# RWKV's low-rank products in fp32r on 128 stacked rows, and part of the down weights' sums made in the score stage of a hybrid GDN/RWKV-7 block

## The chip, the cores and the metric

One core of one Trainium2 chip (trn2). The metric is device time in microseconds of one launch; lower is better. The profile comes from one execution of its own, read by the hardware profiler; the times come from other runs without it.

## The reference, cut to what matters

One layer of an encoder on 512 tokens of width 2048, all in fp32. A norm and one input projection feed two groups of mixers, gated DeltaNet (8 heads of 128) and RWKV-7 (16 heads of 64); then an output projection, cross attention to 256 memory tokens, and an MLP of width 8192 with squared ReLU.

```python
xn = rmsnorm(h); y = xn @ w_in
mixed = concat(gdn_group(y[..., :GDN_COLS]), rwkv_group(y[..., GDN_COLS:]))
h = h + mixed @ w_out
h = h + cross_attention(rmsnorm(h), rmsnorm(mem))
h = h + square(relu(rmsnorm(h) @ mlp_w_up)) @ mlp_w_down
out = rmsnorm(h)
# in rwkv_group: y is mixed with its shifted self, then
w_log = -softplus(-(w0 + tanh(w_lo) @ w2)) - 0.5     # w_lo: 64 columns of y, w2: 64 x 1024
a = sigmoid(a0 + a_lo @ a2)                          # a_lo: 64 columns of y, a2: 64 x 1024
g = sigmoid(g_lo) @ g2
```

## The kernel before, in words

Nearly all large products are made in fp32r, a form of fp32 with fewer bits that TensorE takes at a higher rate. An operand is split into a high part (a cast on ACT) and a low part (a subtraction on DVE), and three products (high by high, high by low, low by high) are added up in PSUM. Small products of the mixers stay in fp32.

The stages follow each other on PE: input projection in 59 blocks of 128 columns (tiles `py`), with the mixers' small products between; key products `kp` and `kq`; value products `vp`, `vo`; output projection `op` (a Strassen form with 7 products); scores `sc`; attention `at`; up (tiles with u at the end) and down (with d at the end), both in the seven-product form too.

In the mixers, and again in up and down, the order of all instructions is written out by hand: chains of work (generators) yield operations, and a planner issues the one that its costs and due times put first (`cost`, `start`, `issue`, `run`). In between (output projection, scores, attention) the program is written straight and the framework's scheduler orders each engine's queue.

RWKV works in 8 head pairs, `rwkv(j)`. Its front end makes two products of 64 rows, `pW` (w2's columns of the pair by tanh(w_lo)) and `pA` (a2's by a_lo): `lw` holds w2 on rows 0 to 63 and a2 on rows 64 to 127, and `wa` the two activations likewise. `rows()` makes `wa` once, from block 0 of the projection. Tiles of one tag share buffers: `sr` has two, `E1`, `tA` and the others one. `rs` are the small products of the recurrence along the eight chunks of 64 tokens.

The seven-product form of down needs four sums of weight blocks (s1 to s4) in 13 groups of 2048 columns; the sums of three more groups are made in place by `insitu`, and `splits` cuts them. `presum` fetches the four blocks A11, A21, A22, A12 of a piece, makes the sums on DVE and stores them to HBM (`Sd`); `todo` and `upto` hold what is left. Most groups are made beside the mixers in pieces of 410 columns (tiles `ds`); `remaining` makes the rest beside up and down in buffers that stand free there (`ab`, `h`, `sl`, `acc`). Down's loads fetch the sums from HBM.

The score stage has two halves g of eight steps n2. A step loads 1024 columns (`kqr`, two DMAs of 256 KB), splits them into `kqh` and `kql` (three buffers each of load and split), and makes 24 products. In the first half each of six steps also splits two blocks of the normed input (`second`); in the second half the first half's softmax and its transposes lie between. Attention's first two loads (`VOd`) follow.

Of the kernel before, what the change touches and what calls it, by code (L numbers as in the profile page):

```python
# [9 lines left out]
F32 = mybir.dt.float32  # L10
F32R = mybir.dt.float32r
# [6 lines left out]
P = 128  # L18
# [6 lines left out]

CST = {}
_off = 0
for _n, _w in (("ident", 128), ("ones", 128), ("mA", 128),
               ("lv64", 2 * 64), ("cen", 64), ("sneg", 128), ("mbias", 128),
               ("rst64", 512)):  # L30
    CST[_n] = (_off, _w)
    _off += _w
# [13 lines left out]
def constants():  # L46
    c = np.zeros((P, NCST), np.float32)

    def put(name, a):
        o, w = CST[name]  # L50
        c[:, o:o + w] = a

    i = np.arange(P)
    put("ident", np.eye(P))
    put("ones", 1.0)
    j = np.arange(64)
    st = (j[:, None] < j[None, :]).astype(np.float32)
    inc = (j[:, None] <= j[None, :]).astype(np.float32)
    put("mA", np.tile(np.concatenate([st, inc], 1), (2, 1)))

    def level(n, s):
        a = np.arange(n)
        blk = a[:, None] // (2 * s) == a[None, :] // (2 * s)
        return (blk & (a[:, None] % (2 * s) >= s) & (a[None, :] % (2 * s) < s)).astype(np.float32)

    put("lv64", np.concatenate([np.tile(level(64, 16 << l), (2, 1)) for l in range(2)], 1))
    put("cen", np.tile(np.eye(64) - 1.0 / 64, (2, 1)))
    put("sneg", -(i[:, None] < i[None, :]).astype(np.float32))
    put("mbias", np.where(i[:, None] <= i[None, :], 1e30, -1e30))
    put("rst64", np.tile((np.arange(512) % 64 != 0).astype(np.float32), (P, 1)))  # L70
    return c


def build(tc, I, out):
# [12 lines left out]

    prm = pc.tile([P, NPRM], F32, name="prm")
    nc.sync.dma_start(prm, I["prm"])
    NC0 = 256  # L90
    cst0 = pc.tile([P, NC0], F32, name="cst0")
    cst = pq.tile([P, NCST - NC0], F32, name="cst")

    def K(name):
        o, w = CST[name]
        return cst0[:, o:o + w] if o < NC0 else cst[:, o - NC0:o - NC0 + w]

# [5 lines left out]
        o, w = PRM[name]  # L103
        return prm[:, o:o + w]

    ident, ones = K("ident"), K("ones")

    def cbias(v, nm):
        t = pc.tile([P, 1], F32, name=f"cb_{nm}")
# [172 lines left out]
    def after(*ev):  # L282
        return lambda: ev in events
# [236 lines left out]
    dp = pq.tile([P, 28], F32, name="dp")  # L520
    omu, nA = dp[:, 0:27], dp[:, 27:28]
    hw0, ha0, hka, hgnw, hconv = (cols(n) for n in ("w0", "a0", "ka", "gnw", "conv"))
    onesr = pq.tile([P, P], F32R, name="onesr")
    bonesr = pq.tile([P, P], F32R, name="bonesr")

    def derived():
        yield DV.tensor_scalar(out=omu, in0=cols("mu"), scalar1=-1.0, scalar2=1.0, op0=ALU.mult, op1=ALU.add)
        for t in (hw0, ha0, hka, hgnw, hconv):
            yield DV.tensor_scalar(out=t, in0=t, scalar1=0.5, scalar2=None, op0=ALU.mult)
        yield after("consts")  # L530
        yield DV.tensor_copy(onesr, ones)
        yield DV.memset(bonesr.bitcast(F32), 0.0)
        for h in (slice(0, 64), slice(64, 128)):
            yield DV.tensor_copy(bonesr[h, h], ones[h, h])
# [126 lines left out]
        yfree.append(ys.pop(n))  # L661


    wa = pq.tile([P, T], F32, name="wa")
    sgh, sgl, sst = (pq.tile([P, T], F32R, name=n) for n in ("sgh", "sgl", "sst"))
    RT = pq.tile([P, 4, 3, 8], F32, name="RT")
    Rd = pd.tile([64, T], F32, name="Rd", tag="Rd")
# [1 line left out]
    def rows():  # L669
        R = tl("gE")  # L670
        yield DV.memset(R, 0.0)
        rs128 = tl("bon")
        g8 = slice(32, 40)
        b8 = slice(64, 72)
        yield after("rstd")
        yield AC.activation(nA, col("alog"), AF.Exp)
        yield DV.tensor_scalar(out=nA, in0=nA, scalar1=-1.0, scalar2=None, op0=ALU.mult)
        yield DV.memset(rs128[g8, :], 1.0)
        for c in range(4):
            yield DV.memset(rs128[g8, c * P:c * P + 1], 0.0)  # L680
        yield after("derived")
        yield from shiftmix(0, 0, wa)
        yield AC.activation(wa[0:64, :], wa[0:64, :], AF.Tanh)
        sg1, y2 = tl("gAq"), tl("gkt")
        yield from shiftmix(1, 1, sg1)
        yield AC.activation(sg1, sg1, AF.Tanh, scale=0.5)
        yield DV.tensor_scalar(out=sg1, in0=sg1, scalar1=0.5, scalar2=0.5, op0=ALU.mult, op1=ALU.add)
        yield from split_(sg1, sgh, sgl)
        events.add(("lowrank",))
        yield from shiftmix(2, 2, y2)  # L690
        yield AC.activation(y2[0:32, :], y2[0:32, :], AF.Tanh, scale=0.5)
        yield AC.activation(R[b8, :], y2[b8, :], AF.Tanh, scale=0.5)
        yield DV.tensor_scalar(out=y2[0:32, :], in0=y2[0:32, :], scalar1=0.5, scalar2=0.5,
                               op0=ALU.mult, op1=ALU.add)

        yield AC.copy(sst[0:32, :], y2[0:32, :])
        yield AC.copy(sst[64:96, :], y2[0:32, :])
        yield DV.tensor_tensor(out=y2[0:32, :], in0=y2[0:32, :], in1=sst[0:32, :].bitcast(F32), op=ALU.subtract)
        yield AC.copy(sst[32:64, :], y2[0:32, :])
        x_, e_ = short(t="st"), tl("gkn")  # L700
        yield DV.tensor_scalar(out=x_[g8, :], in0=y2[g8, :], scalar1=col("dtb")[g8, :], scalar2=None, op0=ALU.add)
        yield DV.scalar_tensor_tensor(out=e_[g8, :], in0=x_[g8, :], scalar=-1.0, in1=x_[g8, :],
                                      op0=ALU.mult, op1=ALU.min)
        yield AC.activation(e_[g8, :], e_[g8, :], AF.Exp)
        yield AC.activation(e_[g8, :], e_[g8, :], AF.Ln, bias=b_one[g8, :])
        yield DV.scalar_tensor_tensor(out=x_[g8, :], in0=x_[g8, :], scalar=0.0, in1=e_[g8, :],
                                      op0=ALU.max, op1=ALU.add)
        yield DV.tensor_scalar(out=x_[g8, :], in0=x_[g8, :], scalar1=nA[g8, :], scalar2=None, op0=ALU.mult)
        yield DV.tensor_tensor_scan(out=R[g8, :], data0=rs128[g8, :], data1=x_[g8, :], initial=0.0,
                                    op0=ALU.mult, op1=ALU.add)  # L710
        R3 = R.rearrange("p (c t) -> p c t", t=P)
        tail = tl("gqn")
        t3 = tail.rearrange("p (c t) -> p c t", t=P)
        yield DV.tensor_tensor(out=t3[g8], in0=R3[g8, :, P - 1:P].broadcast_to([8, 4, P]),
                               in1=R3[g8], op=ALU.subtract)
        yield AC.activation(R[96:104, :], tail[g8, :], AF.Exp)
        yield DV.tensor_scalar(out=R[b8, :], in0=R[b8, :], scalar1=0.5, scalar2=0.5, op0=ALU.mult, op1=ALU.add)
        pt = psb("prt", "scg", 1)
        for c in range(4):
            yield TE.transpose(pt[:, c * P:(c + 1) * P], R[:, c * P:(c + 1) * P], ident)  # L720
        yield SY.dma_start(Rd, R[32:96, :])
        yield DV.tensor_copy(RT, pt.rearrange("p (c a b) -> p c a b", a=4, b=32)[:, :, 1:4, 0:8])
# [135 lines left out]
    def rwkv(j):  # L858
        base = 3 + 7 * j
        js = slice(j * P, (j + 1) * P)  # L860
        lw = tl("lw", P)
        yield SM.dma_start(lw, I["w2a2"][:, js])
        c3 = lambda a: a.rearrange("p (c t) -> p c t", t=64)
        yield after("lowrank")
        yield after("zeros")
        pW, pA = psb(f"pW{j}"), psb(f"pA{j}")
        yield [TE.matmul(pW, lw[0:64, :], wa[0:64, :], start=True, stop=True),
               TE.matmul(pA, lw[64:128, :], wa[64:128, :], start=True, stop=True)]
        tw = short()
        yield AC.activation(tw, pW, AF.Tanh, scale=0.5, bias=hw0[:, j:j + 1])  # L870
        tA = tl("tA")
# [811 lines left out]
    def turned():  # L1683
        g, _, probs = turn.pop(0)
        for e in range(2):
            for mt in range(2):
# [4 lines left out]
                S.copy(phi[kk], pt)  # L1691
                V.tensor_tensor(out=plo[kk], in0=pt, in1=phi[kk].bitcast(F32), op=ALU.subtract)

    for g in range(2):
        banks = (("mm", 2), ("mg", 2), ("mg", 2), ("mm", 2)), (("scr", 1), ("scg", 1), ("mx", 2), ("mx", 2))
        pts = [psb(f"sc{g}_{t}", *banks[g][t]) for t in range(4)]
        for n2 in range(8):
# [3 lines left out]
                nc.sync.dma_start(raw[:, i * 512:(i + 1) * 512], KQd[2 * n2 + i][:, g * 512:(g + 1) * 512])  # L1701
            wh = pw.tile([P, 1024], F32R, tag="whi", name=f"kqh{cnt[0]}", bufs=NWS)
            wl = pw.tile([P, 1024], F32R, tag="wlo", name=f"kql{cnt[0]}", bufs=NWS)
            split(raw, wh, wl)
            if g == 0 and n2 < 6:
                second(2 * n2 + 4)
                second(2 * n2 + 5)
# [15 lines left out]
        if g == 1:  # L1723
            for n in range(2):
                begun.append((psb(f"at{n}", "mg"), *wload(VOd[0][:, :, n * P:(n + 1) * P])))
                attend(*begun[n], 0)
        turn.append((g, pts, []))
        if g == 1:
            for t in range(4):
# [203 lines left out]
    def splits():  # L1933
        for u in units:
            if u[0] == "d" and u[1:3] in INSITU and u[1:] not in PRE:
                for i, w in order_of(u):
                    for x in xs(u):
# [2 lines left out]
                        halves[u, i, x] = hl = yield from take(hfree)  # L1940
                        yield from cut(r, *hl)
                        events.add(("half", u, i, x))
                        if w not in (A11, "s2") and (w != A12 or u == units[-1]):
                            wfree.append(r)
                continue
# [422 lines left out]
def layout(inputs):  # L2368
# [53 lines left out]
    put("alog", a["gdn_A_log"][0].reshape(8, 1), slice(32, 40))  # L2422
    d["prm"] = prm
    d["cst"] = constants()
    d["w2a2"] = np.concatenate([a["rwkv_w2"][0], a["rwkv_a2"][0]], 0)
    g2 = a["rwkv_g2"][0]
    d["g2a"] = np.ascontiguousarray(g2[:128])
    d["g2b"] = np.ascontiguousarray(g2[128:])
# [37 lines left out]
```

## Time and profile before

| | |
|---|---|
| runs | 2888.92, 2887.84, 2888.71 us; median 2888.71 |
| profiled execution | span 2890.0 us from the first to the last instruction; this is the time of it that is on hand, 1.3 above the median of the runs |
| busy | PE 2862.2, PEld 2419.1, DVE 2333.9, ACT 1571.7, POOL 214.7 us |
| DMA | 553.01 MB, mean 191 GB/s |
| granted TensorE clock | 0.999 |
| first and last start on PE | py 6.8 to 907.0; sc 1455.3 to 1544.9; at 1545.2 to 1634.5; first up product 1634.8 |

PE makes the products and PEld loads their weights beside it. A row of a group has the line, engine, operation, tiles as out<-in, shapes and count, then busy time and mean length in ns, then the engine's idle time ahead of it and who ended that. L257 is the planner's helper that records every operation, L122 the helper for products outside it; so rows are told apart by tiles. Rows in order of time have the start, the length, the engine and the operation; SPq is the queue of DMA issues. A row of waits has who waited for whom, the total in us, the count and the longest.

### The profile page before, as it was taken

To read this page: it belongs to the slowest core of one execution; us is meant where nothing else is said; L and a number is where in the kernel's file an instruction comes from. 1 tells how busy PE (TensorE), PEld (TensorE's weight loads), DVE (VectorE), ACT (ScalarE), POOL (GpSimd) and SP (SyncE) were. 2 spreads that over 40 slices of the span, in tenths; PEclk is the share of its full clock that TensorE was granted. 3 is DMA by queue.
4 is the path that set the end of the run, shared out by engine and by line. 5 is a ranking of instruction groups with operands and counts; after the bars stand their busy time and mean duration, and the time that the engine had idled before them with its cause. 6 is when DMAs were issued, how large, how long until landed. Compare 5 with 4: busy or idle time off the path is not lost.

```text
span 2890.0 us, 49168 instructions
## 1 busy us (share of the span) xinstructions
PE 2862.2 (99%) x18794; PEld 2419.1 (84%) x18794; DVE 2333.9 (81%) x3559; ACT 1571.7 (54%) x2233; POOL 214.7 (7%) x539
## 2 busy tenths in 40 slices
PE   9999999999999999999999999999999999999998
PEld 7877887877877888889988888888888888888887
DVE  7787787787877877769956898899998878786888
ACT  6555555645656655664445556555555644454544
POOL 0213213213212100000000000000000000000000
PEclk9999999999999999999999999999999999999999
DMA  5656656657656788784422354666565878887733
GB/s 191 166 147 176 176 149 187 165 154 189 180 161 200 214 257 274 232 292 151 124 95 88 110 164 153 199 195 207 189 200 178 292 249 277 295 257 247 265 101 110
DMA packets 321212, 553.01 MB, mean 191 GB/s; under 512 B 101128, under 2 KB 188428, under 8 KB 320976
## 3 DMA queue, kind: packets, MB, share of 16 engines
q1 hardware_dynamic: 293584, 518.41, 58.7%
q10 hardware_dynamic: 27392, 31.46, 3.1%
q8 instruction: 147, 2.41, 0.3%
q14 instruction: 89, 0.73, 0.1%
HBM read 443.45 MB, written 106.31 MB: 190 GB/s over the span
## 4 chain that ended last, share of the span: by engine, by line
PE 94%; DMA 3%; DVE 1%; ACT 1%; issue 1%; ACTq 0%; SPq 0%; DVEq 0%
PE py L257 22%; PE mxu L257 12%; PE mgd L257 6%; PE mgu L257 6%; PE mxd L257 6%; PE op L122 6%; PE vp L122 3%; PE mmu L257 3%; PE sc L122 3%; PE at L122 3%; PE scrd L257 3%; PE scgd L257 3%; PE mmd L257 3%; PE kq L257 3%; PE kp L257 2%; DMA wraw<-in_wo 1%
## 5 line engine op out<-in xcount | busy, mean ns | idle before, releaser
L257 ACT CAST whi<-wraw 128x1024 fp32r<-128x1024 f32 (+1 forms) x365 | 382.8, 1049 | 370.1 <-PE py L257 138.7
L257 DVE TENSOR_TENSOR wlo<-wraw,whi 128x1024 fp32r<-128x1024 f32 (+1 forms) x365 | 446.8, 1224 | 90.0 <-ACT whi L257 82.5
L257 PE MATMUL py<-xhi,whi 128*128 128x512 f32 x928 | 373.9, 403 | 6.8 <-ACT xhi L257 6.8
L257 PE MATMUL py<-xhi,wlo 128*128 128x512 f32 x928 | 373.1, 402 | 0.0
L257 PE MATMUL py<-xlo,whi 128*128 128x512 f32 x928 | 372.4, 401 | 0.0
L257 ACT CAST whi<-w 128x1024 fp32r<-128x1024 f32 x178 | 187.6, 1054 | 174.0 <-PE scgd L257 42.3
L257 DVE TENSOR_TENSOR wlo<-w,whi 128x1024 fp32r<-128x1024 f32 x178 | 217.3, 1221 | 43.4 <-ACT whi L257 40.9
L257 PE MATMUL mxu<-cb,whi 128*128 128x512 f32 x1016 | 249.3, 392 | 0.0
L257 PEld LDWEIGHTS mxu<-cb,whi 128*128 128x128 f32 x1016 | 184.7, 189 | 34.3
L257 PEld LDWEIGHTS py<-xhi,whi 128*128 128x128 f32 x928 | 175.3, 189 | 42.0 <-ACT xhi L257 6.8
L257 PEld LDWEIGHTS py<-xhi,wlo 128*128 128x128 f32 x928 | 175.3, 189 | 34.7 <-issue 1.0
L257 PEld LDWEIGHTS py<-xlo,whi 128*128 128x128 f32 x928 | 175.3, 189 | 33.8 <-DVE xlo L257 0.5
L131 DVE TENSOR_TENSOR wlo<-wraw,whi 128x1024 fp32r<-128x1024 f32 x112 | 136.7, 1222 | 44.8 <-ACT whi L130 44.3
L130 ACT CAST whi<-wraw 128x1024 fp32r<-128x1024 f32 x112 | 117.6, 1051 | 86.8 <-PE op L122 26.2
L257 PE MATMUL mxu<-cb,wlo 128*128 128x256 f32 x1016 | 142.7, 283 | 0.7 <-DVE wlo L257 0.7
L257 PEld LDWEIGHTS mxu<-cb,wlo 128*128 128x128 f32 x1016 | 135.1, 191 | 6.0 <-DVE wlo L257 0.9
L257 PE MATMUL mgu<-cb,whi 128*128 128x512 f32 x512 | 129.3, 394 | 0.1
L257 PE MATMUL mxd<-whi,cb 128*128 128x512 f32 x512 | 126.8, 389 | 0.0
L257 PE MATMUL mgd<-whi,cb 128*128 128x512 f32 x512 | 126.4, 389 | 0.0
L257 ACT ACT_TABLE_LOAD x87 | 111.6, 1283 | 16.5 <-DVE suml_gon L257 8.6
L122 PE MATMUL op<-ob,whi 128*128 128x256 f32 (+1 forms) x752 | 115.2, 304 | 0.0
L257 ACT CAST whi<-ws 128x1024 fp32r<-128x1024 f32 x75 | 79.0, 1053 | 64.0 <-PE mgu L257 48.1
(943 smaller groups left out, 6429.3 us busy)
## 6 DMA issues: line engine op xcount, KB each, us to landing
wraw<-in_w_in SPq DMA_DIRECT2D x116, 512.0 KB, 4.7
wraw<-in_w_up SPq DMA_DIRECT2D x65, 512.0 KB, 3.6
w<-in_w_up SPq DMA_DIRECT2D x63, 512.0 KB, 4.2
ds<-in_w_dm SPq DMA_DIRECT2D x128, 205.0 KB, 4.4
sd_s<-ds SPq DMA_DIRECT2D x128, 205.0 KB, 4.9
wraw<-sd_s SPq DMA_DIRECT2D x51, 512.0 KB, 4.9
w<-sd_s SPq DMA_DIRECT2D x50, 512.0 KB, 5.5
w<-in_w_dm SPq DMA_DIRECT2D x48, 512.0 KB, 4.9
```

What stands on the lines that cost most here:

```text
L122: PE.matmul(o, l, r, start=start, stop=stop, skip_group_check=again)
L130: S.copy(hi, src)
L131: V.tensor_tensor(out=lo, in0=src, in1=hi.bitcast(F32), op=ALU.subtract)
L257: f(*a, **k)
```

## The change

Three things change. The low-rank operands are split: `xw2` holds the high part of tanh(w_lo) on rows 0 to 63 and its low part on rows 64 to 127, `xa2` the same for a_lo with the halves swapped. The weights are sent twice on the rows (`w2a2` now 128 x 2 x 1024 with w2 and a2 beside each other), and each pair splits its 256 columns into `lhl`. For pW and for pA two fp32r products of 128 rows are added up: low weights, then high weights. `lw` moves into E1's buffer, `wa` into tA's, `lhl` into one of sr's.

Second, the score stage makes up to fifteen pieces of 256 columns of the sums that are left: `fetched` loads, `summed` adds one step later, `stored` writes them in the step after. `remaining` finds fewer left.

Third, smaller edits: the constant of ones is written by a memset into the fp32r tile `onesr` and no longer loaded, and in the in-situ units the buffer of s1 is given back only after s2 is made.

```diff
@@ constants @@
-for _n, _w in (("ident", 128), ("ones", 128), ("mA", 128),
+for _n, _w in (("ident", 128), ("mA", 128),
...
-    NC0 = 256
+    NC0 = 128
...
-    ident, ones = K("ident"), K("ones")
+    ident = K("ident")
+    onesr = pc.tile([P, P], F32R, name="onesr")
+    ones = onesr.bitcast(F32)
+    V.memset(ones, 1.0)
...
-        yield DV.tensor_copy(onesr, ones)
@@ rows @@
-    wa = pq.tile([P, T], F32, name="wa")
+    xw2, xa2 = (pq.tile([P, T], F32R, name=n) for n in ("xw2", "xa2"))
...
+        wa = tl("tA")
+        lo64, up64 = slice(0, 64), slice(64, 128)
         yield from shiftmix(0, 0, wa)
-        yield AC.activation(wa[0:64, :], wa[0:64, :], AF.Tanh)
+        yield AC.activation(wa[lo64, :], wa[lo64, :], AF.Tanh)
+        for X, p, q in ((xw2, lo64, up64), (xa2, up64, lo64)):
+            yield AC.copy(X[p, :], wa[p, :])
+            yield DV.tensor_tensor(out=X[q, :], in0=wa[p, :], in1=X[p, :].bitcast(F32), op=ALU.subtract)
@@ rwkv @@
-        lw = tl("lw", P)
-        yield SM.dma_start(lw, I["w2a2"][:, js])
+        lw = tl("E1", shape=[P, 8, 65]).rearrange("p a b -> p (a b)")[:, 0:2 * P]
+        yield SM.dma_start(lw.rearrange("p (a b) -> p a b", b=P), I["w2a2"][:, :, js])
...
-        yield [TE.matmul(pW, lw[0:64, :], wa[0:64, :], start=True, stop=True),
-               TE.matmul(pA, lw[64:128, :], wa[64:128, :], start=True, stop=True)]
+        lhl = tile_of(pm, [P, 512], F32R, "sr", f"lhl_{cnt[0]}", NSH["sr"])
+        yield from split_(lw, lhl[:, 0:2 * P], lhl[:, 2 * P:4 * P])
+        for i, (pt, X) in enumerate(((pW, xw2), (pA, xa2))):
+            for s in (1, 0):
+                yield TE.matmul(pt, lhl[:, (2 * s + i) * P:(2 * s + i + 1) * P], X, start=s == 1, stop=s == 0)
@@ scores @@
+    spans = [(e, m, c, min(c + M, 2048)) for e, m in todo for c in range(upto.get((e, m, "s4"), 0), 2048, M)]
+    held, made_ = [], []
+    def fetched(s):
+        e, m, c, n = spans.pop(0)
+        b = [pl.tile([P, M], F32, tag=f"ds{i}", name=f"ds{s}_{i}", bufs=2)[:, 0:n - c] for i in range(4)]
+        for i in (A21, A22, A11, A12):
+            nc.sync.dma_start(b[i], I["w_dm"][e, m][i][:, c:n])
+        held.append((e, m, c, n, b))
+    def summed():
+        e, m, c, n, (a11, a21, a22, a12) = held.pop(0)
+        for j, o, x, y, op in (("s1", a22, a21, a22, ALU.add), ("s3", a21, a11, a21, ALU.subtract),
+                               ("s2", a11, a22, a11, ALU.subtract), ("s4", a12, a12, a11, ALU.subtract)):
+            V.tensor_tensor(out=o, in0=x, in1=y, op=op)
+            made_.append((Sd[e, m, j][:, c:n], o))
+            upto[e, m, j] = n
+        if n == 2048:
+            todo.remove((e, m))
+    def stored():
+        while made_:
+            nc.sync.dma_start(*made_.pop(0))
...
+            stored()
+            if g * 8 + n2 < 15:
+                fetched(g * 8 + n2)
             split(raw, wh, wl)
+            if g * 8 + n2:
+                summed()
...
                 attend(*begun[n], 0)
+            stored()
@@ splits, in-situ units @@
+                        if w == "s1":
+                            yield after("sum", u, "s2", x)
@@ layout @@
-    d["w2a2"] = np.concatenate([a["rwkv_w2"][0], a["rwkv_a2"][0]], 0)
+    w2a2 = np.stack([a["rwkv_w2"][0], a["rwkv_a2"][0]], 1)
+    d["w2a2"] = np.concatenate([w2a2, w2a2], 0)
```

More of the change, by code (lines that the diff above doesn't have):

```diff
@@ L54, in constants @@
     put("ident", np.eye(P))
-    put("ones", 1.0)
     j = np.arange(64)
@@ L522, in build @@
     hw0, ha0, hka, hgnw, hconv = (cols(n) for n in ("w0", "a0", "ka", "gnw", "conv"))
-    onesr = pq.tile([P, P], F32R, name="onesr")
     bonesr = pq.tile([P, P], F32R, name="bonesr")
@@ L866, in rwkv @@
         pW, pA = psb(f"pW{j}"), psb(f"pA{j}")
-        yield [TE.matmul(pW, lw[0:64, :], wa[0:64, :], start=True, stop=True),
-               TE.matmul(pA, lw[64:128, :], wa[64:128, :], start=True, stop=True)]
+        cnt[0] += 1
+        lhl = tile_of(pm, [P, 512], F32R, "sr", f"lhl_{cnt[0]}", NSH["sr"])
[3 more added lines that the diff above has]
+                yield TE.matmul(pt, lhl[:, (2 * s + i) * P:(2 * s + i + 1) * P], X, start=s == 1, stop=s == 0)
         tw = short()
```

## The prediction

> **What bounds the kernel now.** I read the table of busy time by stage first, then the waits of PE, then the order of time around the products that change, then DVE and SP in the score stage.
>
> The table's columns are stretch, length, then busy time and instructions of PE, PEld, DVE, ACT and POOL, the granted clock, the DMA share and GB/s. The eight stretches are mixers with input projection, key products, value products, output projection, scores, attention, up, down.
>
> ```profile
> 0.00:907.00 907.00, 897.84 (x7882) 719.72 (x7883) 706.48 (x1305) 502.67 (x708) 199.33 (x508) 1.00 0.62 172
> ...
> 1118.00:1295.50 177.50, 176.55 (x896) 150.73 (x897) 123.27 (x199) 109.27 (x181) 0.00 (x0) 1.00 0.80 261
> ...
> 1455.20:1545.10 89.90, 89.90 (x410) 74.63 (x410) 37.86 (x61) 32.75 (x54) 0.00 (x0) 1.00 0.31 98
> ...
> 1634.60:2271.00 636.40, 635.61 (x3789) 566.10 (x3788) 572.64 (x761) 361.98 (x507) 0.00 (x0) 1.00 0.59 185
> 2271.00:2890.00 619.00, 608.83 (x2687) 503.79 (x2685) 504.49 (x607) 310.11 (x379) 0.00 (x0) 0.99 0.71 234
> ```
>
> PE is busy to within 1 us in every stretch but the first and the last (start and tail of the kernel), at clock 1.00. DVE is 90% busy in the up stage and 42% in the score stage. A busy PE can still hide waits, so the waits of PE come next, first to 1120 us, then from there to the end:
>
> ```profile
> PE py L257 <- ACT xhi L257: 6.8, 1, 6.8
> PE kp L257 <- DVE wlo L257: 2.7, 1, 2.7
> PE rs L257 <- DVE Qs L257: 2.2, 2, 1.2
> PE gs L257 <- DVE TtG L257: 1.2, 1, 1.2
> PE kq L257 <- DVE y L257: 1.1, 1, 1.1
> ...
> PE mxu L257 <- DVE wlo L257: 0.7, 1, 0.7
> PE vo L122 <- DVE wlo L131: 0.7, 1, 0.7
> PE at L122 <- ACT phi L1691: 0.2, 1, 0.2
> ```
>
> The last three are all there is after 1120 us: 1.6 us, of which 0.7 in up, none in down, none in the score stage. So PE's own instructions set the end. Work taken from DVE or from the DMA queues gains at most these few us; work given to them costs nothing until PE waits.
>
> **The low-rank products.** PE in order of time (start, length) at the first head pair and at the third:
>
> ```profile
> 58.37 0.39 PE L257 MATMUL py<-xlo,whi 128*128 128x512 f32 x1
> 58.69 0.69 PE L257 MATMUL pW<-wa,lw 64*128 64x512 f32 x1
> 58.70 0.69 PE L257 MATMUL pA<-wa,lw 64*128 64x512 f32 x1
> 59.22 0.59 PE L257 MATMUL pW<-wa,lw 64*128 64x512 f32 x1
> 59.23 0.59 PE L257 MATMUL pA<-wa,lw 64*128 64x512 f32 x1
> 59.75 0.50 PE L257 MATMUL py<-xhi,wlo 128*128 128x512 f32 x1
> 60.08 0.39 PE L257 MATMUL py<-xhi,whi 128*128 128x512 f32 x1
> 60.31 0.40 PE L257 MATMUL py<-xlo,whi 128*128 128x512 f32 x1
> ...
> 266.84 0.69 PE L257 MATMUL pW<-wa,lw 64*128 64x512 f32 x1
> ...
> 267.90 0.43 PE L257 MATMUL rs<-BK,BTz 128*128 128x64 f32 x2
> 268.15 0.48 PE L257 MATMUL py<-xhi,whi 128*128 128x512 f32 x1
> 268.46 0.39 PE L257 MATMUL py<-xlo,whi 128*128 128x512 f32 x1
> ```
>
> An fp32 product stands as two records. pW and pA start 10 ns apart, so they run together on the two halves of the rows. Neighbouring py start 0.23 us apart (60.08 to 60.31) though each record lasts 0.39: a full fp32r product of 512 columns costs 0.23 of PE's time, its length overlaps. From 58.37 to 60.08 there would be two such intervals without the visit, 0.46; it took 1.71, so the visit costs 1.25. The third visit, between small fp32 products, costs at least the 1.06 from 266.84 to 267.90.
>
> New: four fp32r products of 128 rows and 512 columns, 4 x 0.23 = 0.92. Beside small fp32 products the first one pays what py pays at 268.15, 0.31 instead of 0.23, so 1.00. The saving is 0.06 at worst (1.06 - 1.00) and 0.33 at best (1.25 - 0.92); over 8 head pairs 0.5 to 2.6 us. I take 0.3 per visit, 2.4 us: nearest the first visit, since the fp32r quartet fits between py without a switch on either side.
>
> The Trainium skill, "TensorEngine Tiling (Array Packing)", section Tiling Modes, says that a change of the tiling mode drains the array. This trace agrees: 0.32 into the visit at 58.37 and 0.33 behind it, against 0.23.
>
> The preparation: each head pair now splits 256 columns of weights on ACT and DVE, and the start makes two casts and two subtractions of 64 rows.
>
> ```profile
> L257 ACT CAST khl<-y 128x256 fp32r<-128x256 f32 x16 | 6.5, 407 | 1.8 <-DVE y L257 1.7
> L257 DVE TENSOR_TENSOR sl<-sl,mxu 128x256 f32<-128x256 f32 x34 | 14.3, 420 | 2.5 <-PE mxu L257 0.7
> ...
> 57.40 0.62 ACT L257 CAST sgh<-gAq 128x512 fp32r<-128x512 f32 x1 [1.10 <-DVE gAq L257]
> 58.06 0.69 DVE L257 TENSOR_TENSOR sgl<-gAq,sgh 128x512 fp32r<-128x512 f32 x1 [0.69 <-ACT sgh L257]
> ```
>
> So 8 x 0.41 = 3.3 us of ACT and 8 x 0.42 + 2 x 0.69 = 4.7 us of DVE, in a stage where DVE idles 907 - 706 = 201 us. What hides it is py, which PE has at hand all the time. The first pW comes up to 2 x (0.62 + 0.69) = 2.6 us later for the split of wa, and no PE work is short by it. If DVE is just then late for the recurrence, PE can wait as it does for Qs and TtG above. By those rows I bound this at 2 us either way (another order can also remove such a wait) and take 0. The low-rank weights double to 128 KB a load, on SP, long ahead; they share the buffer of E1, whose old content is read early in the pair before; 0.
>
> The constants: one memset of 128 columns replaces a quarter of a first load and a copy; DVE has nothing to do before x lands, PE starts at 6.8 us behind ACT; 0.
>
> **The sums moved into the score stage.** Fifteen pieces of 256 columns: each 4 loads and 4 stores of 128 KB on SP and 4 DVE operations of 0.42. DVE gets 60 x 0.42 = 25 us more and has 89.9 - 37.9 = 52 us idle there. The DMAs get 120 x 128 KB = 15.7 MB, 175 GB/s over 89.9 us, 273 with the 98 of now; the value stage ran 261 GB/s at a share of 0.80 with 0.7 us of PE waits. What is late next is the queue. Rows on it: the cast of a split on ACT, DVE and SP in order of time, then DMA issues with size and median time to landing.
>
> ```profile
> L130 ACT CAST whi<-wraw 128x1024 fp32r<-128x1024 f32 x112 | 117.6, 1051 | 86.8 <-PE op L122 26.2
> ...
> 1472.95 1.23 DVE L131 TENSOR_TENSOR kql<-kqr,kqh 128x1024 fp32r<-128x1024 f32 x1 [4.22 <-ACT kqh L130]
> 1478.35 1.22 DVE L131 TENSOR_TENSOR kql<-kqr,kqh 128x1024 fp32r<-128x1024 f32 x1 [4.17 <-ACT kqh L130]
> ...
> 1421.17 0.80 SPq L1701 DMA_DIRECT2D kqr<-kqd  x2
> 1422.51 0.33 SPq L1389 DMA_DIRECT2D wraw<-in_w_out  x1
> 1430.93 0.80 SPq L1701 DMA_DIRECT2D kqr<-kqd  x2
> 1434.62 3.54 SPq L1613 DMA_DIRECT2D sl<-in_xT  x2
> ...
> kqr<-kqd SPq DMA_DIRECT2D x27, 256.0 KB, 3.1
> h<-in_w_dm SPq DMA_DIRECT2D x24, 128.0 KB, 3.3
> sd_s<-h SPq DMA_DIRECT2D x24, 128.0 KB, 4.9
> sd_s<-ab SPq DMA_DIRECT2D x40, 256.0 KB, 2.7
> ```
>
> A step of the stage is 24 products, 24 x 0.227 = 5.4 us, and DVE's splits come at that distance with 4.2 idle; 1.7 of sums fit. The split at 1472.95 is the sixth, done at 1474.2, and its products start at 1455.2 + 5 x 5.44 = 1482.4: DVE has a lead of 8.2 us over PE. SP issues ten DMAs a step at about 0.4, 4 of 5.4 us. In the text the next step's load stands behind the stores, which wait for sums, and behind a fetch into one of two buffers, which waits for stores to land. But outside the hand-ordered parts the queue does not keep the order of the text: two score loads (1421, 1431) went before loads of the output projection that the text has ahead of them (1422, 1434). I take 0 and keep +15 (below) as the other end.
>
> **Where the sums leave.** Eight of the thirteen groups of sums are made in the mixers; of the other five, 20 pieces of 512 columns, the score stage takes 7.5, some 30 DVE operations of 512 columns. They lay under PE: at most the 0.7 of wait in up is won; I take 0. The wait added behind the cut of s1 in the in-situ units holds the next cuts of that list until the sum s2 is made, which needs only B11's split, done before; 0, and with the cover gone one DVE operation of about 1.2 us.
>
> **Sum.** -2.4, all from PE in the first 830 us. The profiled execution has a span of 2890.0, 1.3 above the median of the runs; 2890.0 - 2.4 = 2887.6 for the profile, 2888.7 - 2.4 = 2886.3 for the median. A change below 0.2% (5.8 us) counts here as none.
>
> **Rivals.**
> (1) *The score stage's queue becomes a loop.* If SP keeps the order of the text, two steps form a ring: landing of the load 3.1, cast 1.05 and split 1.22, four sums 1.7, landing of the store 4.9, four fetch issues 1.6, the load's second issue 0.4: 14.0, or 7.0 a step against 5.4. Over 15 steps that is 23 us, less the lead of 8.2: +15, 2901. It decides once the ring is over 2 x (5.4 + 8.2/15) = 12 us; with stores landing in 2.7 it is 11.8 and the effect is nil. For it: the text's order, and a DMA rate that goes from 98 to 273 GB/s and lengthens landings. Against: SP's rows above. Chance 0.10.
> (2) *The waits of the first stages shrink.* Another order around the mixers could remove kp's 2.7, kq's 1.1, Qs's 2.2 and TtG's 1.2: with the 2.4 this is -9.6, 2879. Against it: DVE and ACT only get more work there. Chance 0.04.
> (3) *The quartet costs its length, not its interval.* Four products of 0.39 are 1.56 against 1.06 to 1.25, +0.3 to +0.5 a pair, up to +4: 2893. Against: py's intervals, and all four write only two banks as py's do one. Chance 0.05. The Trainium skill's page named above, section Theoretical Speedup, speaks for this side: up to 2x from tiling a contraction of 64 rows, which the change gives up; the pair's 10 ns shows that the old form had it.
> (4) *Nothing moves:* the planner sets the four products apart between small fp32 ones and each pays 0.08: 1.24 a pair, no gain, 2888.7. Chance 0.15.
>
> **How the numbers follow.** My forecast (0.66) gives 2886.3, with 2884 to 2889 for the bounds of PE's term (-2.6 to -0.5) and the 2 us of order. Rivals 3 and 4 and most of this lie within 0.2%: same 0.85. Slower is rival 1 and mixer waits grown: 0.10; faster is rival 2: 0.05. The range 2881 to 2895 holds all but those and the far end of each.
>
> **What would show it.** Right: pW and pA each as two records of 128x512 fp32r, 0.23 apart, and the first py stretch some 2 us shorter; DVE in the score stage at 63 us with PE still unbroken; score loads on SP between fetches; no stores of sums from sl or acc in the down stage; PE's waits after 1120 us below 3 us. Wrong: PE waiting for kql in the score stage, with SP waiting for ds stores ahead of a kqr load; new waits of rs or gs for DVE in the mixers; or PE's instruction time in the first stage unchanged.

## The result, and the profile after

The changed kernel takes 2913.54 us in the median (2913.17 to 2921.15); the kernel before, beside it, 2888.92. The ratio is 1.0091, 95% interval 1.0078 to 1.0103; by the medians it is 24.6 us slower, where 2.4 us less was forecast. The profiled execution has a span of 2917.9, 27.9 above the one of before. On record it is the run of 2919.72, one of the two longer of the five, so the stage lengths below add up to 27.9 and not to 24.6. The kernel before itself ran at 2888.7 to 2893.6 on the chips used below, so times of different comparisons meet through their ratios, and stage lengths through the profiles.

The table of busy time by stage, after (columns as in the prediction): mixers, key products, query products, scores, down.

```profile
0.00:904.60 904.60, 896.15 (x7880) 723.19 (x7881) 697.98 (x1294) 499.86 (x713) 196.86 (x508) 1.00 0.55 162
904.60:1036.20 131.60, 115.96 (x993) 98.74 (x993) 97.98 (x176) 68.78 (x106) 14.81 (x32) 0.94 0.63 190
1036.20:1135.10 98.90, 96.84 (x549) 84.48 (x548) 64.97 (x107) 55.92 (x101) 0.00 (x0) 0.97 0.79 249
...
1472.20:1572.50 100.30, 92.53 (x410) 76.58 (x409) 60.49 (x121) 32.98 (x54) 0.00 (x0) 0.95 0.74 234
...
2297.70:2917.90 620.20, 609.43 (x2689) 504.31 (x2687) 497.74 (x595) 310.58 (x379) 0.00 (x0) 1.00 0.67 225
```

The same table, before, for the key and the query products:

```profile
907.20:1022.30 115.10, 109.94 (x990) 94.43 (x989) 96.08 (x174) 65.73 (x104) 15.39 (x31) 1.00 0.68 205
1022.30:1118.20 95.90, 94.37 (x548) 82.28 (x547) 68.11 (x112) 55.65 (x101) 0.00 (x0) 1.00 0.87 272
```

Three stages carry the loss: key products 115.1 to 131.6 (+16.5), query products 95.9 to 98.9 (+3.0), scores 89.9 to 100.3 (+10.4); the mixers gained 2.1 (first py 6.8 to 907.2 before, 6.3 to 904.6 after). Up and down kept their lengths (635.6 both times; 619.6 and 620.2). In each of the three, PE is longer idle (length less PE's busy time: 5.2 to 15.6, 1.5 to 2.1, 0 to 7.8), and its busy time grows too, at a granted clock of 0.94 to 0.97. PE's waits, after:

```profile
PE ptr L1698 <- DVE plo L1701: 7.8, 1, 7.8
...
PE kp L259 <- ACT mhl L259: 4.2, 2, 2.5
PE gn L259 <- DVE suml_gn L259: 3.4, 1, 3.4
PE rs L259 <- DVE BK L259: 3.1, 1, 3.1
```

The first is in the score stage, the others are among the key products. ACT there, in order of time (in brackets the idle time ahead and who ended it):

```profile
909.26 1.04 ACT L259 CAST whi<-wraw 128x1024 fp32r<-128x1024 f32 x1 [6.35 <-PE kp L259]
...
910.52 0.51 ACT L259 ACTIVATE mhl<-mraw,prm 128x256 fp32r<-128x256 f32 x1
910.93 0.60 ACT L259 CAST sumh_gn<-sg 128x512 fp32r<-128x512 f32 x1
```

ACT's queue holds a cast of key weights, which waits 6.35 us for a key product to give its buffer back; the casts behind it, sumh_gn and mhl among them, are what PE waits for next. PE and ACT stand behind each other through ACT's order. The quartet itself, first head pair:

```profile
61.08 0.40 PE L259 MATMUL py<-xlo,whi 128*128 128x512 f32 x1
61.32 0.62 PE L259 MATMUL pW<-xw,lhl 128*128 128x512 f32 x2
61.78 0.63 PE L259 MATMUL pA<-xa,lhl 128*128 128x512 f32 x2
62.24 0.39 PE L259 MATMUL py<-xhi,wlo 128*128 128x512 f32 x1
```

From py to py 1.16, less the one interval of 0.23 that would stand there anyway: the visit costs 0.93, where the old one cost 1.25.

### The profile page after: what moved, and what is told of

The parts are those of the page before. It is cut to its first block, busy times and chain, and to the rows that moved or that the text cites. A ratio compares the mean times of both kernels' runs of the same rounds, so it can differ in the third digit from the quotient of the medians.

```text
span 2917.9 us, 49333 instructions
## 1 busy us (share of the span) xinstructions
PE 2871.2 (98%) x18794; PEld 2431.1 (83%) x18794; DVE 2339.6 (80%) x3593; ACT 1571.5 (54%) x2241; POOL 211.7 (7%) x539
## 4 chain that ended last, share of the span: by engine, by line
PE 92%; DMA 4%; DVE 2%; ACT 1%; issue 1%; SPq 1%; ACTq 0%; DVEq 0%
PE py L259 23%; PE mxu L259 12%; PE mgd L259 6%; PE mgu L259 6%; PE mxd L259 6%; PE op L124 5%; PE vp L124 3%; PE mmu L259 3%; PE at L124 3%; PE scrd L259 3%; PE scgd L259 3%; PE mmd L259 3%; PE kq L259 3%; PE kp L259 2%; PE vo L124 2%; DMA sd_s<-ds 1%
```

## The experiments

Three places had to be explained, so there were three theories. **A**: the splits of lw and wa make the front of each head pair late, and the end of the last pair meets the key products. **B**: in the score stage the queue is a ring of fetch, sum and store over two buffers. **C** came up with the first runs: the mixers make fewer sums now, and what they leave costs time in the down stage.

**The two halves alone.** `low` has the low-rank products, their preparation, the constants and the in-situ wait, without `fetched`, `summed` and `stored`. `score` has only those three and the in-situ wait, with the old products.

> The kernel before with the change's low-rank products, their preparation and the constants; the score stage has no sums. Theory A (the split of lw and the later wa delay the front of each head pair, and the last pair's recurrence is no longer covered by the key products; independent of the sums in the score stage): key stage near 131 us instead of 115.1, score stage at 89.9, time 2888.9 + 14 to 17 = 2903 to 2906. Rival (the longer key stage comes from the sums: with seven groups of them instead of eight made in the mixers the planner puts other work there): key stage near 115 and time near 2886.5, the 2.4 us of the quartet won.

> The kernel before with only the sums of the score stage (and the wait that goes with them in the up stage); low-rank products as before. Theory B (the queue is a ring of loads, sums and stores): score stage 100 us instead of 89.9, splits of the score weights 6 to 6.8 us apart, PE waits near 8 us for plo at the first transposes, key stage at 115; time 2888.9 + 10 to 12 = 2899 to 2901. Rival (the score stage is late because the low-rank change made everything before it late, its cost comes with that alone): score stage 90, time near 2889.

`low`: ratio 1.0136 (1.0121 to 1.0151), far over what either expected. Table of busy time: mixers with key products, scores, down.

```profile
6.40:1033.10 1026.70, 1010.68 (x8872) 820.85 (x8873) 793.46 (x1456) 565.64 (x815) 208.87 (x528) 0.99 0.57 166
...
1468.80:1558.70 89.90, 89.90 (x410) 74.56 (x410) 37.85 (x62) 32.74 (x54) 0.00 (x0) 1.00 0.32 99
2283.90:2929.80 645.90, 612.44 (x2689) 505.73 (x2687) 517.36 (x627) 310.23 (x379) 0.00 (x0) 0.98 0.72 241
```

The key stage is long without any sums in the score stage (129.6 us), so the first loss belongs to the low-rank part, as A said. But down is 26 us longer than before. PE's longest wait of `low`, then ACT in order of time:

```profile
PE scrd L259 <- ACT whi L259: 22.4, 1, 22.4
...
2773.14 1.04 ACT L259 CAST whi<-wraw 128x1024 fp32r<-128x1024 f32 x1 [27.73 <-DMA wraw<-sd_s]
```

The cast waits 27.7 us for a load of sums that are not made yet. Loads of blocks for the sums that down makes itself, with their counts, before and then `low`:

```profile
sl<-in_w_dm SPq DMA_DIRECT2D x21, 256.0 KB, 6.1
acc<-in_w_dm SPq DMA_DIRECT2D x7, 256.0 KB, 6.6
```

```profile
sl<-in_w_dm SPq DMA_DIRECT2D x36, 256.0 KB, 5.5
acc<-in_w_dm SPq DMA_DIRECT2D x12, 256.0 KB, 6.1
```

At four loads a piece that is 7 pieces of 512 columns before and 12 in `low`: up to the end of the key products the mixers made 34 pieces of 410 columns (136 loads of `ds`) instead of 40 (160).

`score`: ratio 1.0043 (1.0028 to 1.0058), 11.8 us by the medians. Mixers with key products, then scores:

```profile
6.40:1022.70 1016.30, 1008.76 (x8873) 815.06 (x8873) 799.07 (x1466) 566.04 (x807) 211.88 (x528) 1.00 0.62 175
...
1458.00:1559.60 101.60, 92.05 (x410) 76.28 (x409) 61.02 (x121) 32.96 (x54) 0.00 (x0) 0.95 0.76 232
```

The score stage is late with old products and an undisturbed key stage (117.3): B holds, its rival falls. The two halves are not additive: +1.36% and +0.43% alone, +0.91% together, because the score stage's sums are what spares down the 26 us.

**Is it the lateness?** Two edits of one number, by how long the planner reckons the weights of a pair to be under way before their use:

```diff
-        yield SM.dma_start(lw, ...)                            # SM: 8000 ns
+        yield Lane(nc.sync, "SP", margin=11400.0).dma_start(lw, ...)   # front_late, on the kernel before
+        yield Lane(nc.sync, "SP", margin=3000.0).dma_start(lw..., ...)  # low_m3, on low
```

> The kernel before with one number changed: the planner reckons the low-rank weights to land 3.4 us later (11400 ns instead of 8000), so pW and pA come that much later in every pair and nothing else is asked of any engine. Theory A (it is the lateness of the front): the last pair ends later, key stage 5 to 17 us longer than 115.1, time 2894 to 2906. Rival A2 (it is the added instructions on ACT and DVE, or their place in the in-order queues, not the lateness): within 3 us of 2888.9.

> As the run with the low-rank products alone, and the planner reckons their weights to land after 3000 ns instead of 8000 (they land 4.2 us after the issue in the trace). Theory A: the front comes up to 5 us earlier than in that run and the key stage goes back to about 115 us; 2886 to 2889. Rival A2: key stage and time as in that run, 2903 to 2906.

`front_late`: ratio 1.0002 (0.9993 to 1.0012): for the rival. `low_m3`: key stage 112.0, about as A expected, with every added split in it; so the added instructions don't cost the key stage its time. Its ratio is 1.0051 all the same, for down still waits 10.2 us for sums (40 loads, 10 pieces). A was then narrowed: lateness costs once too little time is left between the last pair's products and the first key product.

> The kernel before with the planner's landing time of the low-rank weights at 13000 ns instead of 8000, nothing else. Theory A' (a later front costs only once the last pair's recurrence starts its last products less than some 15 us ahead of the first key product; in the runs so far 15 to 19 us cost nothing, 8.6 cost 11 to 14 us): the lead shrinks from 18.2 to 12 to 15, the stretch from the first input projection product to the first query product is 1016 to 1024 long, 2889 to 2897. Rival A2 (the added splits on ACT and DVE cost it, not the lateness): 1015.5 as before, 2889.

`late2`: ratio 1.0042 (1.0026 to 1.0059), so lateness alone, with the old products, can cost 12 us. (Its executions spread more than those of any other kernel here, from 2898.7 to 2918.1; the profiled one took 2908.3.) But not where A put it: the key stage is 115.4, and the loss is in the mixers (912.5 instead of 900.4), one wait in each of several pairs, two of them:

```profile
PE gi1u L257 <- DVE TtG L257: 3.1, 1, 3.1
PE gi3u L257 <- DVE TtG L257: 2.8, 1, 2.8
```

**The sums that are left.** On the kernel before, with the in-situ wait of the change:

```diff
-            chain(presums(..., PIECE, after("kp", 15)),
+            chain(presums(..., PIECE, after("kp", 0)),
```

> The kernel before, but the planner stops to make sums at the first key product, so four pieces fewer of 410 columns are made ahead (about 36 of 40) and the rest is left to the up and down stages; the in-situ wait of the change is in. Theory C (the loss of the low-rank run in the down stage is the sums that its mixers did not make: 12 pieces left there cost 23 us, 10 pieces 11, 7 none): 11 pieces left, PE waits 12 to 20 us in the down stage for a cast that waits for a load of sums, 2901 to 2909. Rival (the stall comes from the in-situ wait or from the low-rank change itself): 2889.

Ratio 1.0038 (1.0027 to 1.0048); 37 pieces are made ahead and 10 left for down, and one wait stands there:

```profile
PE scrd L257 <- ACT whi L257: 10.1, 1, 10.1
```

So C is shown with the old products: the count of the pieces is enough, and the in-situ wait is not the cause, for `score` has it too and its down stage is 619.6. Over all runs, down's length goes by the pieces left to it: 619.6 to 620.5 with up to 9, 632 to 633 with 10, 646 with 12.

**The ring.** `score_3buf` is `score` with

```diff
-        b = [pl.tile([P, M], F32, ..., bufs=2)...]
+        b = [pl.tile([P, 192], F32, ..., bufs=3)...]      # and spans in steps of 192
```

> As the run with only the score stage's sums, but pieces of 192 columns instead of 256 and three buffers instead of two, so a fetch waits for stores issued a step earlier and not for those just ahead of it. Theory B (the ring over two buffers): score stage 90 to 93 us instead of 101.6, PE's wait at the first transposes under 3, time 2889 to 2893. Rival (the DMAs or DVE are loaded too much, whatever the buffers): score stage 97 or more, 2898 or more.

Ratio 1.0001 (0.9991 to 1.0011), score stage 89.9. SP's waits for stores of sums to land, in `score`, then in `score_3buf`:

```profile
SPq L1701 <- DMA sd_s<-ds: 17.2, 13, 2.5
```

```profile
SPq L1701 <- DMA sd_s<-ds: 0.7, 1, 0.7
```

As many pieces pass, so the number of instructions on SP and DVE is not the cause. The pieces are a quarter narrower too, and three buffers of 256 columns were not tried; so the run alone doesn't tell the third buffer from the fewer bytes. SP's waits for stores speak for the buffer.

**Both mended, and one at a time.** `mended` is the change with margin 3000 and pieces of 128 columns in three buffers; `change_3buf` has only three buffers (192 columns), `change_m3` only the margin.

> The whole change with three numbers of it altered: the landing of the low-rank weights reckoned at 3000 ns, score pieces of 128 columns in three buffers. If theories A, B and C are all of the loss: stretch to the first query product 1014 to 1016, score stage 90, no wait for sums in the down stage (about 37 pieces made in the mixers, 3.75 pieces of 512 columns in the score stage, 6 left for down), time 2885 to 2890. Rival (something else in the change costs): above 2893.

> The whole change, but with score pieces of 192 columns in three buffers; the planner's landing time stays at 8000. If the ring and the late front are separate causes: score stage back to 89.9 (the change: 100.3), the stretch to the first query product stays near 1030, no wait for sums in down (12 pieces left by the mixers less 5.6); 2913.5 - 10.4 = 2901 to 2905. Rival (they are one: the score stage recovers and something later gives it back): 2911 or more.

> The whole change, but with the planner's landing time of the low-rank weights at 3000; score pieces stay at 256 columns in two buffers. If the causes are separate: stretch to the first query product 1014 to 1018, score stage 100 to 102; 2913.5 - 13 = 2899 to 2902. Rival (the score stage's loss follows from the late mixers): score stage near 90, 2890.

| kernel | first py to first kq | scores | down | ratio |
|---|---|---|---|---|
| before | 1015.5 | 89.9 | 619.6 | |
| the change | 1029.9 | 100.3 | 620.2 | 1.0091 (1.0078 to 1.0103) |
| change_3buf | 1029.2 | 90.0 | 620.3 | 1.0066 (1.0051 to 1.0081) |
| change_m3 | 1015.4 | 103.8 | 620.2 | 1.0068 (1.0052 to 1.0085) |
| mended | 1017.8 | 90.1 | 620.2 | 1.0003 (0.9994 to 1.0013) |

Each edit takes away its own stage's loss and leaves the other's: two causes. Together they bring the change back to the time of before, not under it: `mended` took 2893.99 us, more than the 2885 to 2890 expected, but the kernel before took 2892.62 beside it. The times of the two single edits came out 5 to 7 us above what was expected: the gains were taken from the stages of the longer, profiled execution, but subtracted from the median. The profiled spans fell by 9.9 and 11.4, by 25.9 with both. Alone they fell short because other stages grew against the change: the score stage by 3.5 with the margin alone, the value and output products by 2.9 there and by 1.9 with three buffers alone.

**What is it in the mixers?** If the margin only sets how early the front comes, 4500 on the kernel before and 5000 on the mended change should help:

> The kernel before with the planner's landing time at 4500 instead of 8000, nothing else. Theory A as a matter of lead alone: the front comes 3.5 us earlier, PE's waits in the key stage (5.2 us idle) shrink, 2885 to 2888. Rival (what counts is the order the planner then finds, and any move of the front can cost): 2889 or more, with waits in other places.

> As the mended change, with 5000 instead of 3000 (in the traces the weights land 4 to 6 us after the issue). If the mended run's remaining waits in the mixers (pW for its split 1.6, ri7s 1.7, clock at half for 3.4 us at 165 us) come from weights reckoned too early: first stretch 3 to 6 us shorter than 905.9 and 2886 to 2889. Rival (any order has its own few us): 2890 to 2896.

Both came out slower, 1.0020 (1.0010 to 1.0030) and 1.0040 (1.0025 to 1.0055). The first is as its rival had it; the second, at 2902.0 us, lies beyond its rival's range too. So two more numbers were put on each curve, one execution each, to tell a shift by the added splits (D) from a scatter of the order that the planner finds (S):

> The kernel before, planner's landing time 6500 instead of 8000. Theory S (the order found scatters, with any products): stretch from the first input projection product to the first query product anywhere between 1014 and 1028, not on a line between 4500 (1020.7) and 8000 (1015.5). Theory D (the added splits are the cause, the old kernel is smooth): 1016 to 1020.

> The kernel before, planner's landing time 10000. Theory S: anywhere from 1014 to 1028. Theory D: 1015 to 1016, as at 8000 and 11400.

> The whole change with pieces of 192 columns in three buffers, planner's landing time 6500. Theory S: anywhere from 1014 to 1030, so it may well lie under 1021. Theory D: between 5000 (1021.1) and 8000 (1029.2), 1023 to 1027.

> The whole change with pieces of 192 columns in three buffers, planner's landing time 10000. Theory S: anywhere from 1014 to 1030. Theory D: above 1029, later still.

First py to first value product (to the first query product in brackets), us, from the profiles:

| margin, ns | old products | new products |
|---|---|---|
| 3000 | | 1109.6, 1110.9, 1112.8 (1014.6, 1015.4, 1017.8) |
| 4500 or 5000 | 1114.8 (1020.7) | 1119.4 (1021.1) |
| 6500 | 1115.5 (1021.7) | 1123.5 (1025.9) |
| 8000 | 1111.4, 1112.9, 1110.6 (1015.5, 1016.3, 1014.4) | 1125.1, 1126.9, 1128.8 (1026.7, 1029.2, 1029.9) |
| 10000 | 1114.4 (1023.0) | 1112.4 (1015.6) |
| 11400 | 1109.9 (1015.5) | |
| 13000 | 1125.9 (1027.9) | |

From kernel to kernel with the same products and margin it moves by some 2 to 4 us; from margin to margin by 16 with the old and 19 with the new. Each figure is of one execution, and 10 of the old's 16 rest on 13000 (`late2`). The old has no direction; the new rises from 3000 to 8000, as D would have it, and then drops. The new at 10000 speaks against D: there the last pair's pW starts at 839.7 us, later than the change's 835.6, and the stretch is 16 us shorter. It is one execution, but with 2895.3 us it is 11 under the shortest of the same kernel at 8000 (`change_3buf`, 2906.7 to 2910.3).

```profile
6.80:1118.20 1111.40, 1102.33 (x9418) 896.61 (x9418) 868.26 (x1577) 621.36 (x908) 212.29 (x528) 1.00 0.64 184
```

```profile
6.30:1135.10 1128.80, 1108.95 (x9419) 906.41 (x9419) 858.50 (x1562) 621.73 (x916) 209.23 (x528) 0.99 0.58 173
```

```profile
7.00:1119.40 1112.40, 1103.09 (x9418) 901.81 (x9418) 864.22 (x1574) 622.83 (x916) 210.56 (x528) 1.00 0.61 180
```

That is before, the change, and the new products at 10000, over this stretch: PE executes the same number of products in all three, to within one record. The margin of 8000, carried over from the old front, meets a bad order with the new one. Which step of the order decides it stays open: the waits stand in another place in each bad one. Whether the splits or the shared buffers (`lw` in E1's, `wa` in tA's, `lhl` in one of sr's) shift the order was not separated.

**A version under both?** Stopping the sums at the first key product shortened that stretch in `fewer_sums` (1106.8), so it was joined with three buffers of 192 columns, with old products and with new ones at 3000.

> The kernel before with old low-rank products; the planner stops to make sums at the first key product, and the score stage makes 15 pieces of 192 columns in three buffers. The run with fewer sums had a stretch of 1011.6 to the first query product, 3.9 less than before, and lost it to 11 us in the down stage; here 10 pieces less 5.6 are left for down, so that wait goes: 2888.9 - 4 = 2885, ratio 0.9975 to 0.9995. Rival (the 3.9 was scatter of the order): ratio 1.000 or more.

> The whole change with the landing time 3000, sums stopped at the first key product, score pieces of 192 columns in three buffers. If stopping the sums there gains 3 to 4 us in the key stage, as with the old products: stretch 1011 to 1014, 2884 to 2888, ratio 0.997 to 0.9995; if the gain was scatter: as the mended change, ratio 1.000.

The stretch was as short as hoped (1106.9 and 1109.4), but with the old products the score stage gave 3.4 back (93.3; PE waits 3.0 for plo again), and the ratios are 1.0003 (0.9995 to 1.0012) and 1.0012 (1.0002 to 1.0022). No kernel here beats the one before.

## Why the prediction was wrong

- **The products: right at the first pair, open in the sum.** 0.92 a visit was forecast, 0.93 measured at the first pair, so rival 3 falls: the length (1.56) was not paid. But the forecast took all eight pairs to be like the first, a quartet between py. At the other seven the planner set small fp32 products between the four, the condition of rival 4, and the fp32r product behind them costs 0.31 to 0.34 again. The fifth pair, PE in order of time:

```profile
500.36 0.39 PE L259 MATMUL pA<-xa,lhl 128*128 128x512 f32 x1
500.59 0.38 PE L259 MATMUL pvt<-cst,gv 128*128 128x128 f32 x2
...
501.12 0.48 PE L259 MATMUL pA<-xa,lhl 128*128 128x512 f32 x1
501.43 0.40 PE L259 MATMUL py<-xlo,whi 128*128 128x512 f32 x1
```

  So the 0.32 and 0.33 around the old visit can't be put down to a change of the tiling mode by this trace: beside small products of 128 rows, with no such change, the price is the same. Of the 2.4 us PE's busy time from the first py to the first value product shows nothing. Where the clock never fell in it, it is 1102.3, 1102.2 and 1101.4 with the old products (before, `score_3buf`, `fewer_sums`) and 1103.0 and 1102.5 with the new (`low_m3`, `change_m3`). The py stretch points to a gain at 8000 (899.0 to 900.4 with the old, 897.1 to 899.2 with the new), but from margin to margin it goes from 895.2 to 906.0 with the new alone. So the term of 2.4 stays unproven. Rival 2 did not occur.
- **The preparation: the step that failed most.** It was costed at 0, bounded at 2 us, since DVE idles 201 us and "no PE work is short by it". The first pW came 2.6 us later, as worked out (3.1 from the first py). What failed is the bound: waits of 2 us seen in one order were taken for the most that another order can do. The engines' queues are one fixed order, and with the margin left at 8000 the one that the planner found cost +16.5 and +3.0 in the key and query products. In the runs the old products, too, move by 16 us with that one number. A reading went with it: "PE is busy to within 1 us in every stretch but the first and the last" does not hold for the key products, where PE was idle for 5.2 of 115.1 us even before, nor for the query products (1.5).
- **The sums that leave: right for before, wrong for the change.** "Eight of the thirteen groups are made in the mixers" was taken as given. With the new products at that margin the mixers make 34 pieces instead of 40; the sums are the work that gets what is over. Down still had five pieces to make (15 loads of `sl`, 5 of `acc`), where the forecast's signs had none. Without the score stage's share down lost 26 us (`low`).
- **The score stage: the wrong value taken.** Rival 1 named the place, the mechanism and +15, and had 0.10; +10.4 came. SP's rows of the output projection were taken as a sign that the queue leaves the order of the text. In the score stage each fetch stayed behind the stores. SP after, one step and the next fetch:

```profile
1504.45 1.76 SPq L1710 DMA_DIRECT2D ds<-in_w_dm  x4
1506.26 0.42 SPq L1734 DMA_DIRECT2D kqr<-kqd  x1
1506.73 1.97 SPq L1725 DMA_DIRECT2D sd_s<-ds  x4
1508.79 0.38 SPq L1734 DMA_DIRECT2D kqr<-kqd  x1
1510.40 1.76 SPq L1710 DMA_DIRECT2D ds<-in_w_dm  x4
```

  Fetch, half a score load, stores, the other half, and a gap of 1.2 until the stores have landed. Every second split on DVE:

```profile
1504.89 1.22 DVE L133 TENSOR_TENSOR kql<-kqr,kqh 128x1024 fp32r<-128x1024 f32 x1 [0.76 <-ACT kqh L132]
...
1517.01 1.23 DVE L133 TENSOR_TENSOR kql<-kqr,kqh 128x1024 fp32r<-128x1024 f32 x1 [0.56 <-ACT kqh L132]
...
1529.90 1.23 DVE L133 TENSOR_TENSOR kql<-kqr,kqh 128x1024 fp32r<-128x1024 f32 x1 [1.77 <-ACT kqh L132]
...
1547.61 0.42 DVE L1717 TENSOR_TENSOR ds<-ds,ds 128x256 f32<-128x256 f32 x1 [1.59 <-DMA sd_s<-ds]
1547.95 1.28 DVE L1701 TENSOR_TENSOR plo<-ptr,phi 128x512 fp32r<-128x512 f32 x2
```

  Two steps take 12.1 and 12.9 us: the rival's 14.0 was too long, its limit of 12 was passed. The term that it had too large is the store's landing, 4.9; in the score stage the stores took 3.2 in the median and the loads 3.6, and with these its sum gives 12.8. PE came to wait not for kql but for plo, which stood on DVE behind a sum that waited for a DMA. DVE's busy time, 60.5 in the stage, and the DMAs' 234 GB/s against 63 and 273 forecast, were near; neither was used up.

The range has a slip that changes nothing: by its own terms the upper end of the forecast is 2888.7 - 0.5 + 2 = 2890.2, not 2889.

## What to carry to other kernels

Where the order is planned, added instructions of 0.4 us can move a stage by much more than their length: here by some 14 us at a margin of 8000, and not at 10000 (1114.4 old, 1112.4 new). Scan the planner's numbers around the change before judging it, and cost it with the scatter that such a scan shows, not with the waits seen in one order. Work that only fills gaps is a budget: ask where it is due when less of it is done. A buffer that is stored and refetched in one step binds its queue to the landing of the store; count the ring, and give it a third buffer.

## What was not expected of the hardware

A wait of PE cost more than its length, for the clock fell behind it. The table for stretches of the change (the first two lines around a wait of 3.1 us among the key products, the third after another wait there, the last at the first transposes):

```profile
987.24:990.65 3.41, 1.06 (x6) 0.92 (x7) 2.47 (x5) 2.64 (x4) 0.00 (x0) 1.00 0.53 179
990.65:994.06 3.41, 3.41 (x13) 2.93 (x12) 2.32 (x6) 1.45 (x2) 0.00 (x0) 0.50 0.59 169
...
919.00:925.80 6.80, 5.04 (x16) 4.21 (x17) 5.33 (x10) 2.90 (x4) 0.00 (x0) 0.50 0.95 292
1543.60:1553.80 10.20, 5.11 (x16) 4.41 (x17) 7.02 (x13) 2.22 (x3) 0.00 (x0) 0.50 0.74 243
```

The clock stood at half for 3.4, 6.8 and 10.2 us, and twice more among the key and query products, for 3.4 us from 912.2 and 6.8 from 1035.0. PE behind the wait for plo, in order of time:

```profile
1548.69 1.97 PE L1698 MATMUL ptr<-cst,pr 128*128 128x128 f32 x8 [7.78 <-DVE plo L1701]
...
1552.16 0.63 PE L124 MATMUL sc<-kql,hh 128*128 128x512 f32 x1
1552.59 0.63 PE L124 MATMUL sc<-kqh,hl 128*128 128x512 f32 x1
...
1554.34 0.40 PE L124 MATMUL sc<-kql,hh 128*128 128x512 f32 x1
1554.57 0.40 PE L124 MATMUL sc<-kqh,hl 128*128 128x512 f32 x1
```

Behind the wait the products start 0.43 apart, later 0.23 again. The score stage's 10.4 us are 7.8 of wait and 2.6 of this; the key stage's 16.5 are 10.5 more of idle time and 6.0 more of busy time. The Trainium skill, "TensorE: Matmul & The Clock Gate", section Part 1, says that the clock goes to half after an idle window of about 3.4 us and comes back after a busy one of that length. This trace agrees in the length, with spells of one, two and three times 3.41 us, but the windows ahead of the falls were not idle: in the 3.41 us before each of the five falls PE was busy for 0.4 to 1.1 us, and in `mended` one fell (at 164.8) behind a window with 1.8. All five falls lie whole multiples of 3.41 us apart, from 912.2 to 1543.6, so the windows seem to run on by themselves and a wait counts by how much of one window it fills. The fall at 990.65 came 1.1 us after PE had begun again behind a wait of 3.1. In the kernel before, a wait of 2.7 brought no fall: counted back from the fall at its end (2883.6), it is split between two windows, with PE busy for 2.2 and 1.9. The prediction priced each wait by its length alone.
